# A sum over channels in the attention: two float32r products of split squares instead of one in float32

## The chip, the cores and the metric

One core of a Trainium2 chip runs the kernel. The metric is device time in microseconds, lower is better: the median of the runs. Beside it one execution is profiled, which tells what each engine did when.

## The reference

A hybrid decoder layer on 256 tokens of 1024 channels, all in float32: a SwiGLU feed-forward block, then a Mamba-2 branch and a differential-attention branch side by side, merged by sigmoid gates, then a second feed-forward block. What is changed lies in the attention branch:

```python
p = jax.nn.softmax(s, axis=-1)
attn = p[:, :, 0] - lam * p[:, :, 1]
return jnp.einsum('bhqk,bkhe->bqhe', attn.astype(v.dtype), v)
...
out = out.transpose(1, 0, 2, 3, 4).reshape(b, L, H, DA_V_DIM)
out = rmsnorm(out, subln_g) * (1.0 - lam_init)
return out.reshape(b, L, DA_WIDTH) @ w_branch
```

There are 8 heads. Each has two softmaxes over scores of 64 channels, and 128 output channels, over which `rmsnorm` takes the mean of the squares.

## The kernel before

Large products are done in float32r with split operands. A float32 tile is rounded to `hi` by a cast on ScalarE (L162 for weights, L186 for activations), `lo` = value - `hi` is made on VectorE (L163, L187), and a product is then three float32r products: hi by hi, hi by lo, lo by hi (L196, L197 and L199 in `mm_t`). Weights stream in from DRAM through three `raw` buffers and are split ahead of their use.

After the first feed-forward block the main stream on TensorE is one projection after another, each through `mm_t`: `pxs` and `pz` for the Mamba branch, `pq` and `pk` for queries and keys, `pgt` for the gates, `pws` (Mamba branch output) and `pwd` (attention branch output, which reads the attention's result `oh`, `ol`). Small work of the branches is added between these projections by `Background`: a generator such as `att_work` yields estimates in microseconds and is advanced after each projection. In this part of the kernel no hand-written order is kept on the engines: the framework's scheduler places the instructions of each engine, and so decides between which projection products the small ones stand.

`att_work` handles the heads in four pairs `hp`. For each head:

- `psc` (L833, L834): the scores. For each of the two softmaxes m the 64 channels of m lie on 64 of the 128 rows of the array; each m has one product of 128 columns (first block of queries) and one of 256. They are in float32.
- L835 adds the ALiBi bias on VectorE; L839 and L841 find the negated maxima; the exponentials run on ScalarE (L241); L850 to L855 normalise and subtract on VectorE.
- `pa` (L860): three transposes on TensorE, copied to `aT` (L863).
- `po` (L866, L867): the product with the values, in float32. A pair of heads shares one `po` tile, 128 channels by 2 heads x 256 tokens.

Then, once for each pair: the squares `sqo` of `po` on ScalarE (L869), their sum over the 128 channels, which is a product `pno` with a 128x128 tile of ones in float32 (L871), logarithm and exponential on ScalarE (both through L241), the scaling on VectorE (L875), and the split into `oh` and `ol` (L186, L187). The next head's `psc` does not depend on this. After the last pair stands an activation table load (L234) on ScalarE for the part that follows.

`k2` is a pool of 7 buffers of 2 KB a partition, from which `aT` (one for a head) and `sqo` come. `bg` is a pool of 5 PSUM banks, from which `psc`, `pa`, `po` and `pno` come. A float32 matmul runs as two passes, and the profile shows each pass as a matmul of its own with a weight load.

Of the kernel before, what the change touches and what calls it, by code (L numbers as in the profile page):

```python
# [14 lines left out]
F32 = mybir.dt.float32  # L15
F32R = mybir.dt.float32r
# [8 lines left out]
P = 128  # L25
T = 256
# [19 lines left out]
def tile_hybrid_layer(ctx: ExitStack, tc: tile.TileContext, x, ffn1_pre_g, ffn1_w_gate, ffn1_w_up,  # L46
# [4 lines left out]
    nc = tc.nc  # L51
    const = ctx.enter_context(tc.tile_pool(name="const", bufs=1))
# [4 lines left out]
    def k4(shape, name, dt=F32):  # L57
        return sb.tile(shape, dt, tag="k4", name=name, bufs=K4_BUFS)

    def k3(shape, name, dt=F32):  # L60
        return sb.tile(shape, dt, tag="k3", name=name, bufs=K3_BUFS)

    def k2(shape, name, dt=F32):
        return sb.tile(shape, dt, tag="k2", name=name, bufs=K2_BUFS)
# [4 lines left out]
    def tiny(n, name):  # L69
        return sb.tile([P, n], F32, tag=f"tiny{n}", name=name, bufs=10)  # L70
# [9 lines left out]
    def bg(shape, name):  # L80
        return ps.tile(shape, F32, tag="bg", name=name, bufs=5)
# [103 lines left out]
    def split(hi, lo, src):  # L185
        nc.scalar.copy(hi, src)  # L186
        nc.vector.tensor_sub(lo, src, hi.bitcast(F32))  # L187
# [52 lines left out]
    def act(*args, **kw):  # L240
        a = nc.scalar.activation(*args, **kw)  # L241
        if act_fence[0] is not None:
            tc.add_manual_dep(a.ins, act_fence[0], order, reason="activation table")
        act_since.append(a.ins.name)
# [35 lines left out]
    nc.gpsimd.memset(nhalf, -0.5)  # L280
    ones = const.tile([P, P], F32, name="ones")
    nc.gpsimd.memset(ones, 1.0)

    pw = bg([P, P], "warm")

# [535 lines left out]
    def att_work():  # L821
        for hp in range(4):
            po = bg([P, 2, T], f"po{hp}")
            for i in range(2):
                hd = hp * 2 + i
                qh = qT[hd // 4][:, hd % 4, :]
                kh = kT[hd // 4][:, hd % 4, :]

                s = k3([P, 2, 3 * P], f"s{hd}")
                for m in range(2):  # L830
                    ms = slice(m * 64, (m + 1) * 64)
                    psc = bg([P, 3 * P], f"psc{hd}{m}")
                    nc.tensor.matmul(psc[:, :P], qh[ms, :P], kh[ms, :P], start=True, stop=True)  # L833
                    nc.tensor.matmul(psc[:, P:], qh[ms, P:], kh[ms, :], start=True, stop=True)  # L834
                    nc.vector.scalar_tensor_tensor(s[:, m, :], dneg, 2.0 ** -(hd + 1), psc, ALU.mult, ALU.add)  # L835
                yield 0.9
                nm = tiny(6, f"nm{hd}")
                nmv = nm.rearrange("p (m b) -> p m b", b=3)
                nc.vector.tensor_reduce(nm, s.rearrange("p m (b k) -> p (m b) k", k=P), AX.X, ALU.max,  # L839
                                        negate=True)  # L840
                nc.vector.tensor_tensor(nmv[:, :, 1], nmv[:, :, 1], nmv[:, :, 2], ALU.min)  # L841
                sm = tiny(4, f"sm{hd}")
                smv = sm.rearrange("p (m b) -> p m b", b=2)
                blk = (slice(0, P), slice(P, 3 * P))
                for m in range(2):
                    for qb in range(2):
                        act(s[:, m, blk[qb]], s[:, m, blk[qb]], AF.Exp, bias=nmv[:, m, qb:qb + 1],
                            accum_out=smv[:, m, qb:qb + 1])
                yield 1.0
                nc.vector.reciprocal(sm, sm)  # L850
                nc.vector.tensor_scalar(smv[:, 1, :], smv[:, 1, :], nlam, None, ALU.mult)
                for qb in range(2):
                    s0 = s[:, 0, blk[qb]]
                    nc.vector.tensor_scalar(s0, s0, smv[:, 0, qb:qb + 1], None, ALU.mult)
                    nc.vector.scalar_tensor_tensor(s0, s[:, 1, blk[qb]], smv[:, 1, qb:qb + 1], s0, ALU.mult,  # L855
                                                   ALU.add)

                pa = bg([P, 3 * P], f"pa{hd}")
                for i3 in range(3):
                    nc.tensor.transpose(pa[:, i3 * P:(i3 + 1) * P], s[:, 0, i3 * P:(i3 + 1) * P], ident)  # L860
                yield 1.3
                aT = k2([P, 3 * P], f"aT{hd}")
                nc.scalar.copy(aT, pa)  # L863
                hs = slice((hd % 4) * P, (hd % 4 + 1) * P)
                vh = vt[hd // 4]
                nc.tensor.matmul(po[:, i, :], vh[:, 0, hs], aT[:, :T], start=True, stop=False)  # L866
                nc.tensor.matmul(po[:, i, P:], vh[:, 1, hs], aT[:, T:], start=False, stop=True)  # L867
            sq = k2([P, 2, T], f"sqo{hp}")
            nc.scalar.activation(sq, po, AF.Square)  # L869
            pn = bg([P, 2, T], f"pno{hp}")  # L870
            nc.tensor.matmul(pn.rearrange("p a b -> p (a b)"), ones, sq.rearrange("p a b -> p (a b)"),  # L871
                             start=True, stop=True)
            act(sq, pn, AF.Ln, scale=1.0 / P, bias=eps_c)
            act(sq, sq, AF.Exp, scale=-0.5)
            nc.vector.scalar_tensor_tensor(sq, po, g8, sq, ALU.mult, ALU.mult)  # L875
            if hp % 2 == 0:
                oh[hp // 2] = k4([P, 4, T], f"oh{hp}", F32R)
                ol[hp // 2] = k4([P, 4, T], f"ol{hp}", F32R)
            o = (hp % 2) * 2
            split(oh[hp // 2][:, o:o + 2, :], ol[hp // 2][:, o:o + 2, :], sq)  # L880
            yield 1.3
# [46 lines left out]
    for c in range(4):  # L928
# [11 lines left out]
        back.run(BG_US)  # L940

    back.add(att_work())

    def gates(half):
# [100 lines left out]
```

## Time and profile before

| | |
|---|---|
| median of 3 runs | 768.17 us (767.91 to 768.85) |
| profiled execution, own time | 768.8 us |
| its span (first to last instruction) | 766.0 us |
| granted TensorE clock, mean | 0.999 |
| TensorE matmul busy | 751.8 us (98%) |
| VectorE busy | 522.5 us (68%) |
| ScalarE busy | 441.7 us (58%) |
| attention with `psc` to the last `pno` | about 430 to 524 us after the span's start |

In a row of a timeline the columns are: start, duration (both us), engine, line, operation, tile written <- tiles read, shapes, and how many equal ones were merged; in brackets the idle time of the engine before it and what ended it. In a row of a group, durations are minimum/median/maximum in ns. Matmuls are pipelined and overlap, so their starts tell what they hold TensorE for, and their durations don't. In a row of waits: who waited, at which line, for whom; us in total, times, longest.

### The profile page before, as it was taken

How to read it: one execution, taken by the hardware profiler on the slowest of the kernel's cores; microseconds unless marked ns; L12 is line 12 of the kernel's file. 1: busy time of each engine (PE TensorE's matmuls, PEld its weight loads, DVE VectorE, ACT ScalarE, POOL GpSimd, SP SyncE). 2: the span in 40 equal slices, each digit the busy share in tenths (PEclk: the TensorE clock that was granted, in tenths of full speed). 3: DMA queues.
4: the chain of work that ended last, by engine and by line, in shares of the span. 5: the costliest groups of instructions: out<-in, count | busy, mean ns of one | idle time of the engine just before them, and what ended most of it. 6: DMA issues, size and time to landing. Idle time of an engine off the chain costs nothing.

```text
span 766.0 us, 11904 instructions
## 1 busy us (share of the span) xinstructions
PE 751.8 (98%) x4811; PEld 668.9 (87%) x4811; DVE 522.5 (68%) x815; ACT 441.7 (58%) x721; POOL 32.7 (4%) x73
## 2 busy tenths in 40 slices
PE   8899999999999999999999999999999999999996
PEld 6688888888889999899999988989988888888885
DVE  5586677654577888887868777676785767666612
ACT  7475566553566565666836767665573656555511
POOL 3300000000200000000000000000011000000000
PEclk9999999999999999999999999999999999999999
DMA  9576665586253638465535554436481676545801
GB/s 322 131 237 204 220 220 219 172 297 219 62 165 113 214 119 267 145 219 177 182 110 172 160 164 143 133 114 217 171 296 56 200 240 194 173 169 186 296 0 55
DMA packets 104199, 136.97 MB, mean 179 GB/s; under 512 B 2668, under 2 KB 88784, under 8 KB 104144
## 3 DMA queue, kind: packets, MB, share of 16 engines
q1 hardware_dynamic: 101728, 129.51, 51.4%
q0 software_dynamic: 2112, 6.18, 2.6%
q8 instruction: 37, 0.61, 0.3%
q10 hardware_dynamic: 304, 0.53, 0.2%
q14 instruction: 18, 0.15, 0.1%
HBM read 135.13 MB, written 1.08 MB: 178 GB/s over the span
## 4 chain that ended last, share of the span: by engine, by line
PE 88%; DVE 4%; ACT 3%; issue 1%; POOL 0%; DVEq 0%; POOLq 0%; ACTq 0%
PE acc_f L422 16%; PE pup_f L212 9%; PE pg_f L212 9%; PE pn_f L227 4%; PE pg_f L211 4%; PE pup_f L211 4%; PE pn_mx L227 3%; PE acc_mx L422 3%; PE pxs L197 2%; PE pxs L199 2%; PE pxs L196 2%; PE pz L196 2%; PE pz L199 2%; PE pz L197 2%; PE pgt L199 1%; PE pgt L196 1%
## 5 line engine op out<-in xcount | busy, mean ns | idle before, releaser
L163 DVE TENSOR_TENSOR wlo<-raw,whi 128x1024 fp32r<-128x1024 f32 (+1 forms) x246 | 291.2, 1211 | 47.5 <-ACT whi L162 47.1
L162 ACT CAST whi<-raw 128x1024 fp32r<-128x1024 f32 (+1 forms) x246 | 247.1, 1042 | 52.8 <-PE acc_f L422 18.4
L212 PE MATMUL pg_f<-u_f,whi 128*128 128x512 f32 x288 | 101.2, 396 | 0.0
L212 PE MATMUL pup_f<-u_f,whi 128*128 128x512 f32 x288 | 101.1, 396 | 0.0
L211 PE MATMUL pg_f<-u_f,wlo 128*128 128x256 f32 x252 | 70.6, 280 | 0.0
L211 PE MATMUL pup_f<-u_f,wlo 128*128 128x256 f32 x252 | 70.4, 279 | 0.0
L212 PEld LDWEIGHTS pg_f<-u_f,whi 128*128 128x128 f32 x288 | 53.0, 188 | 9.6
L212 PEld LDWEIGHTS pup_f<-u_f,whi 128*128 128x128 f32 x288 | 52.8, 188 | 9.7
L422 PE MATMUL acc_f<-whi,gh_f 128*128 128x512 f32 x176 | 58.2, 390 | 0.0
L422 PE MATMUL acc_f<-wlo,gh_f 128*128 128x512 f32 x176 | 58.2, 390 | 0.0
L422 PE MATMUL acc_f<-whi,gl_f 128*128 128x512 f32 x176 | 58.1, 389 | 0.0
L211 PEld LDWEIGHTS pup_f<-u_f,wlo 128*128 128x128 f32 x252 | 47.6, 189 | 1.6
L211 PEld LDWEIGHTS pg_f<-u_f,wlo 128*128 128x128 f32 x252 | 47.6, 189 | 1.6
L216 DVE TENSOR_TENSOR su_f<-pup_f,su_f 128x256 f32<-128x256 f32 x36 | 15.2, 421 | 39.7 <-ACT su_f L215 39.7
L422 PEld LDWEIGHTS acc_f<-wlo,gh_f 128*128 128x128 f32 x176 | 33.0, 188 | 6.9
L422 PEld LDWEIGHTS acc_f<-whi,gl_f 128*128 128x128 f32 x176 | 33.0, 188 | 6.8
L422 PEld LDWEIGHTS acc_f<-whi,gh_f 128*128 128x128 f32 x176 | 33.1, 188 | 6.7
L197 PE MATMUL pws<-yl,whi 128*128 128x256 f32 x128 | 32.8, 291 | 0.0
L196 PE MATMUL pz<-u_mx,whi 128*128 128x256 f32 x128 | 32.3, 289 | 0.0
L196 PE MATMUL pgt<-u_mx,whi 128*128 128x256 f32 x128 | 32.2, 288 | 0.0
L196 PE MATMUL pws<-yh,whi 128*128 128x256 f32 x128 | 32.0, 285 | 0.0
L197 PE MATMUL pgt<-u_mx,whi 128*128 128x256 f32 x128 | 31.8, 284 | 0.0
(305 smaller groups left out, 1574.1 us busy)
## 6 DMA issues: line engine op xcount, KB each, us to landing
raw<-in_w_in_dram SPq DMA_DIRECT2D x40, 1024.0 KB, 5.5
raw<-in_ffn_w_down_dram SPq DMA_DIRECT2D x22, 1024.0 KB, 5.0
raw<-in_ffn_w_gate_dram SPq DMA_DIRECT2D x20, 1024.0 KB, 5.9
raw<-in_ffn_w_up_dram SPq DMA_DIRECT2D x20, 1024.0 KB, 5.7
raw<-in_ssd_w_branch_dram SPq DMA_DIRECT2D x8, 1024.0 KB, 5.3
acb<-acd POOLq DMA_DIRECT2D x8, 512.0 KB, 4.0
raw<-in_da_w_branch_dram SPq DMA_DIRECT2D x4, 1024.0 KB, 5.3
raw<-in_w_out_dram SPq DMA_DIRECT2D x4, 1024.0 KB, 6.2
```

Of the source, the lines that this page charges most:

```text
L162: nc.scalar.copy(hi[:, js, :], r[:, q * nj + j:q * nj + j + n, :])
L163: nc.vector.tensor_sub(lo[:, js, :], r[:, q * nj + j:q * nj + j + n, :], hi[:, js, :].bitcast(F32))
L196: nc.tensor.matmul(acc[m], wh(j)[:, cs], ah(k0 + j), start=first and j == 0, stop=False)
L197: nc.tensor.matmul(acc[m], wh(j)[:, cs], al(k0 + j), start=False, stop=False)
L199: nc.tensor.matmul(acc[m], wl(j)[:, cs], ah(k0 + j), start=False, stop=last and j == KD - 1)
L211: nc.tensor.matmul(acc[:, :T], wl(j)[:, cs], ah(j), start=False, stop=False)
L212: nc.tensor.matmul(acc, wh(j)[:, cs], ahl(j), start=j == 0, stop=j == KD - 1)
L216: nc.vector.tensor_tensor(dst[:, m, :], acc[:, :T], dst[:, m, :], ALU.add)
L227: nc.tensor.matmul(acc, a(k0 + j), b(j), start=first and i == 0, stop=last and i == 11)
L422: nc.tensor.matmul(acc[b][q], x_[:, ts], w_(kt)[:, halves[q]], start=i == 0 and kt == 0 and x_ is ah and w_ is wh, stop=i == n - 1 and kt ...
```

## The change

A float32r copy of the tile of ones, `ones_r`, is made once on VectorE at the start. For each pair of heads the squares `sq` are split on VectorE: a copy into a float32r tile `sqh` (hi), and a subtraction `sql` = `sq` - `sqh` (lo), both 128x512 and from the pool `k2`. The sum over channels is then two float32r products with `ones_r`, accumulated in the same `pno` tile: hi first, then lo. Everything before and behind stays as it was in the text of the program; the scheduler places all of it anew.

```diff
     ones = const.tile([P, P], F32, name="ones")
     nc.gpsimd.memset(ones, 1.0)
+    ones_r = const.tile([P, P], F32R, name="ones_r")
+    nc.vector.tensor_copy(ones_r, ones)
...
             sq = k2([P, 2, T], f"sqo{hp}")
             nc.scalar.activation(sq, po, AF.Square)
             pn = bg([P, 2, T], f"pno{hp}")
-            nc.tensor.matmul(pn.rearrange("p a b -> p (a b)"), ones, sq.rearrange("p a b -> p (a b)"),
-                             start=True, stop=True)
+            sqh, sql = [k2([P, 2 * T], f"sqo{hp}{x}", F32R) for x in "hl"]
+            sqf = sq.rearrange("p a b -> p (a b)")
+            nc.vector.tensor_copy(sqh, sqf)
+            nc.vector.tensor_sub(sql, sqf, sqh.bitcast(F32))
+            for i, part in enumerate((sqh, sql)):
+                nc.tensor.matmul(pn.rearrange("p a b -> p (a b)"), ones_r, part, start=i == 0, stop=i == 1)
             act(sq, pn, AF.Ln, scale=1.0 / P, bias=eps_c)
             act(sq, sq, AF.Exp, scale=-0.5)
             nc.vector.scalar_tensor_tensor(sq, po, g8, sq, ALU.mult, ALU.mult)
```

The changed program, built, differs in the order of instructions only from the first of these places to the first `pwd` products (and by the copy of the ones at the start of VectorE). With the number of TensorE instructions of each kind in the program's order, around the four places: before, the one `pno` product follows `po` after 7, 6, 6 and 7 float32r products, and at the first three `psc` (L833, L834, L833, L834) follows it directly. After, the hi product follows `po` after 10, 10, 10 and 16 float32r products; at the first three come `psc` L833, L834, then the lo product, then `psc` L833, L834; at the fourth six float32r products and the lo product. On VectorE the copy and the subtraction stand directly behind each other, except at the fourth place, where a product with the gates (L973) lies between.

## The prediction

> **What bounds the kernel now.** I read the page first, then the sums of the stretch in which the attention runs, then the rows of the tiles `pno` and `psc` in order of time, and last the waits there. The profiled execution took 768.8 us, 2.8 us more than its span; the runs have a median of 768.17 us, so it lies 0.6 us above it, within their spread. All sums are made against the span of 766.0 us and carried over to the median.
>
> ```profile
> PE 751.8 (98%) x4811; PEld 668.9 (87%) x4811; DVE 522.5 (68%) x815; ACT 441.7 (58%) x721; POOL 32.7 (4%) x73
> PE 88%; DVE 4%; ACT 3%; issue 1%; POOL 0%; DVEq 0%; POOLq 0%; ACTq 0%
> ```
>
> The first row is busy time by engine, the second the shares of the chain that ended last. TensorE is both times the bound. The attention shows no exception:
>
> ```profile
> core 0: us, PE busy (x) PEld busy (x) DVE busy (x) ACT busy (x) POOL busy (x), PEclk, DMA share, GB/s
> 430.00:530.00 100.00, 98.32 (x767) 90.00 (x766) 72.96 (x129) 70.86 (x138) 0.00 (x0) 1.00 0.47 156
> ```
>
> So a microsecond of TensorE issue saved or added here is a microsecond of the end, while VectorE has 27 us of room in these 100 us and its additions cost only where TensorE waits for them. Four places count, one per pair of heads `hp`.
>
> **TensorE: the sum over channels.** The fourth place (`hp` 3) shows the old product by itself among float32r products:
>
> ```profile
> 522.76 0.28 PE L196 MATMUL pws<-yh,whi 128*128 128x256 f32 x1
> 522.89 1.12 PE L871 MATMUL pno<-sqo,ones 128*128 128x512 f32 x2
> 523.46 0.68 PE L197 MATMUL pws<-yl,whi 128*128 128x256 f32 x1
> 523.97 0.28 PE L196 MATMUL pws<-yh,whi 128*128 128x256 f32 x1
> ```
>
> Columns are start, duration, engine, line. Starts tell more than durations, since matmuls overlap. From 522.76 to 523.97 are 1.21 us, and two 256-column float32r products stand in it besides the old one. These start 0.12 us apart when nothing disturbs them (453.21, 453.32, 453.44 below), so the float32 product, two passes, holds TensorE for 1.21 - 0.24 = 0.97 us. A float32r product of 512 columns:
>
> ```profile
> 552.21 7.96 PE acc_mx L422 x35
> ```
>
> 35 of them in 7.96 us are 0.227 us each, two are 0.45. At `hp` 3 the change saves 0.97 - 0.45 = 0.52 us.
>
> **TensorE: what the new products come between.** At `hp` 0, 1 and 2 the old product is followed at once by the next head's scores, `psc`. Their two halves (m = 0, 1) use 64 rows of the array each:
>
> ```profile
> 453.21 0.28 PE L197 MATMUL pgt<-u_mx,whi 128*128 128x256 f32 x1
> 453.32 0.28 PE L196 MATMUL pgt<-u_mx,whi 128*128 128x256 f32 x1
> 453.44 0.28 PE L197 MATMUL pgt<-u_mx,whi 128*128 128x256 f32 x1
> 453.56 0.28 PE L196 MATMUL pgt<-u_mx,whi 128*128 128x256 f32 x1
> 453.70 1.13 PE L871 MATMUL pno<-sqo,ones 128*128 128x512 f32 x2
> 454.75 0.50 PE L833 MATMUL psc<-k,q 64*128 64x128 f32 x4
> 455.08 0.61 PE L834 MATMUL psc<-k,q 64*128 64x256 f32 x4
> 455.62 0.39 PE L197 MATMUL pgt<-u_mx,whi 128*128 128x256 f32 x1
> 455.84 0.28 PE L196 MATMUL pgt<-u_mx,whi 128*128 128x256 f32 x1
> ```
>
> In the program the order is L833 and L834 of the first half, then both of the second, each two passes. Here all four passes of L833 start before the first of L834: the halves run side by side. In the built changed program they no longer stand together. At each of these three places the order is: hi product, first half of `psc`, lo product, second half. A lo product that takes all 128 rows stands between the halves, so they can't lie over each other. What a half costs by itself the trace doesn't show; the pair by itself it does:
>
> ```profile
> 430.00 0.64 PE L199 MATMUL pgt<-u_mx,wlo 128*128 128x256 f32 x4
> 430.57 0.50 PE L833 MATMUL psc<-k,q 64*128 64x128 f32 x4
> 430.89 0.61 PE L834 MATMUL psc<-k,q 64*128 64x256 f32 x4
> 431.43 0.39 PE L196 MATMUL pgt<-u_mx,whi 128*128 128x256 f32 x1
> 431.65 0.28 PE L197 MATMUL pgt<-u_mx,whi 128*128 128x256 f32 x1
> ```
>
> The last L199 starts at 430.36 (three steps of 0.12). From there to 431.65 are 1.29 us, less 0.24 for two undisturbed products: 1.05 us for a pair, its way in and out included. As its halves lie over each other, a half alone costs the same 1.05 at the upper end. At the lower end it costs what its columns cost in the old product: 0.97 us for 2 x 512 columns, so 0.73 for 2 x 128 + 2 x 256.
>
> One place before: 453.56 to 455.84 is 2.28, less 0.24, so 2.04 us for the old product and the pair. After: 2 x 1.05 + 0.45 = 2.55 at the upper end, 2 x 0.73 + 0.45 = 1.91 at the lower. The place changes by -0.13 to +0.51 us. I take 0.5, because that row is of the very operation, with its entry and exit. TensorE in sum: 3 x 0.5 - 0.52 = +1.0 us (bounds -0.9 and +1.0). The change saves 0.5 us four times and loses about 1.0 three times.
>
> "TensorE: Matmul & The Clock Gate" of the Trainium skill, section "Step-by-step: what each phase is for", says that matmuls stay in program order and only weight loads are pulled ahead. By that rule the halves would already run one after the other and parting them would be free. The rows above speak against it for these two halves. "TensorEngine Tiling (Array Packing)" of the same skill, "Key Properties", says that a change of tiling mode drains the array; the parted order has two more such changes at each place, which is the direction of my sum and no part of it.
>
> **VectorE and the waits.** Added are four copies and four subtractions of 128x512, and one copy of 128x128 at the start, where nothing waits for it. Nearest rows (for a copy: one tensor in, SBUF to SBUF):
>
> ```profile
> L366 DVE TENSOR_SCALAR un_f<-h,r_f x3: 479/501/598, 16.2 to 581.1; 128x512 f32<-128x512 f32 x3
> L187 DVE TENSOR_TENSOR ol<-sqo,oh x4: 680/682/691, 458.4 to 527.9; 128x512 fp32r<-128x512 f32 x4
> ```
>
> 0.50 + 0.68 = 1.18 us a place, 4.7 in all, against 27 us of room. They lie between ScalarE's square and the products, so TensorE may wait. What it waits for now:
>
> ```profile
> PE pa L860 <- DVE s L855: 1.6, 4, 0.6
> PEld pa L860 <- DVE s L855: 0.6, 1, 0.6
> PEld pno L871 <- ACT sqo L869: 0.4, 2, 0.2
> ```
>
> At `hp` 0 the square starts at 453.05 and takes 0.60; VectorE is idle then:
>
> ```profile
> 453.05 0.60 ACT L869 ACTIVATE sqo<-po 128x512 f32<-128x512 f32 x1
> 455.71 0.56 DVE L835 SCALAR_TENSOR_TENSOR s<-dneg,psc 128x384 f32<-128x384 f32 x1 [3.57 <-PE psc L834]
> ```
>
> The copy ends at 453.65 + 0.50 = 454.15. The built order puts three more float32r products ahead of the hi product, so TensorE is there at 453.70 + 0.36 = 454.06: it waits 0.1, and the main projections queued behind it wait too. The lo part comes 0.68 later, which the first half of `psc` (0.73 at least) covers. At `hp` 1 and 2 a split of weights (L163, 1.22 us) may stand before the copy; four more products are the cover there, so 0 to 0.6. I take 0.15 a place, 0.6 in all, less the 0.4 for `pno` that goes: +0.2. The waits for `pa`, 2.2 us now, sit behind the softmax of the head whose second half comes later; `pa` is moved too, so I leave them as they are, with -1 to +1.5 as their bounds.
>
> The square of `hp` 1:
>
> ```profile
> 475.62 0.60 ACT L869 ACTIVATE sqo<-po 128x512 f32<-128x512 f32 x1
> ```
>
> The two new tiles of a place take buffers from the pool `k2`: five a place instead of three, of seven, so a buffer comes round at the next place or the one after it, some 23 us on (453.05 to 475.62), when its last reader, the split of `oh`, is done; nothing is costed for it.
>
> Sum: +1.0 + 0.2 = +1.2 us. Span 767.2, time 768.17 + 1.2 = 769.4 us.
>
> **Rivals.** A, the sum above: 769.4. B, program order: if the halves run one after the other as the program has them, parting them is free and only the products count, 4 x -0.52 + 0.2 = -1.9, so 766.3. Against it stands that two halves one after the other would take 2 x 0.73 = 1.46 us by the lower price, and the whole pair takes 1.05. By the rule of the skill's first page above it would come out as B.
>
> C, the last place turns into a wait. In the built order the last lo product stands six products ahead of the first `pwd`, where the old one stood 43 ahead. From it to the first `pwd` that reads `hp` 3's `oh` are 6 + 21 products (the scheduler has put eight of the second `pwd` in between), 27 x 0.12 = 3.2 us. What must happen meanwhile, as it is now:
>
> ```profile
> 522.74 1.98 ACT L162 CAST whi<-raw 128x1024 fp32r<-128x1024 f32 x2
> 524.62 0.69 ACT L241 ACTIVATE sqo<-pno,eps_c 128x512 f32<-128x512 f32 x1
> 525.34 0.63 ACT L241 ACTIVATE sqo<-sqo 128x512 f32<-128x512 f32 x1
> 525.99 1.28 ACT L234 ACT_TABLE_LOAD   x1
> 527.28 0.62 ACT L186 CAST oh<-sqo 128x512 fp32r<-128x512 f32 x1
> ```
>
> From the first Ln (524.62) to the end of the cast (527.90) are 3.3 us, and the product itself adds 0.23: 3.5, 0.3 too late. Now casts of weights hold the Ln up by 0.6 us more; if one (1.0 us) does so there, `pwd` waits 1.3, with two of them 2.3. Price 0.3 to 2.3; from 0.4 us on it makes the whole slower by over 0.2%. With 1.9 it is 771.3. Against it: the scheduler moved those eight products to cover just this, and one cast has gone ahead of the square.
>
> **How the numbers follow.** A has 0.60, B 0.08, C 0.32. 0.2% is 1.5 us, about what a measurement of this kernel can tell from no change. A at +1.2 with 0.7 either way is within it in about three quarters of its cases and above in the rest; C is above in most. Faster 0.07, same 0.50, slower 0.43. The range: from 767.5 (A with the lower price of the halves, -0.9 + 0.2) to 771.3 (C); B and the longest waits of C lie outside.
>
> **What would show it.** Right: at `hp` 0 to 2 two `psc` groups of L833 x2, L834 x2 instead of x4, with a `pno` start between, and about 2.5 us from the last float32r product ahead to the second after; `pno` as eight products of one pass each, at `hp` 3 two of them in 0.45 us; TensorE waits of a few tenths for the hi copy. Wrong: the second half starts beside the lo product, or a half alone takes clearly under 0.9 us (then less than +1.2, or faster); or a wait over 0.5 us of `pwd` for `oh` (C), or waits for `pa` in sum more than 1.5 us from 2.2.

## The result, and the profile after

The changed kernel takes 770.26 us (median of 7 runs, 769.98 to 770.45), the kernel before 767.91 us beside it (7 runs, 767.54 to 768.85). The ratio is 1.0028 with a 95% interval of 1.0017 to 1.0040: slower by 2.35 us or 0.28%, over the 0.2% that the prediction took for what a measurement can tell. The profiled execution took 770.4 us with a span of 768.5 us.

First the page of the changed kernel: busy time by engine, and the shares of the chain that ended last. Then the sums of the stretch in which the attention runs.

```profile
PE 754.0 (98%) x4811; PEld 670.3 (87%) x4811; DVE 527.1 (69%) x824; ACT 441.7 (57%) x721; POOL 32.6 (4%) x73
PE 89%; DVE 4%; ACT 2%; issue 1%; POOL 0%; DVEq 0%; POOLq 0%; ACTq 0%
...
430.00:530.00 100.00, 98.63 (x753) 90.03 (x751) 74.78 (x134) 67.60 (x134) 0.00 (x0) 1.00 0.44 142
```

TensorE is the bound as before, and its busy time has grown by 2.2 us. VectorE has 4.6 us more, about the 4.7 forecast. These totals do not say where the end moved. The starts do: the first `psc` product starts at 430.57 before and 430.68 after, the first `acc_mx` product (L422, now L424) at 552.05 and 554.44. So the stretch from the one to the other takes 121.48 us before and 123.76 after, +2.28 us. What comes behind it takes 214.0 us before and 214.1 after. Nearly the whole difference lies in the attention's stretch, and each experiment below is given with the length of that stretch.

Now one place, `hp` 0, in the changed kernel's timeline (start, duration, engine, line):

```profile
453.79 0.43 DVE L875 CAST sqo0h<-sqo 128x512 fp32r<-128x512 f32 x1 [1.53 <-ACT sqo L871]
...
454.03 0.28 PE L197 MATMUL pgt<-u_mx,whi 128*128 128x256 f32 x1
...
454.36 0.47 PE L878 MATMUL pno<-sqo0h,ones_r 128*128 128x512 f32 x1
454.76 0.48 PE L835 MATMUL psc<-k,q 64*128 64x128 f32 x2
455.08 0.59 PE L836 MATMUL psc<-k,q 64*128 64x256 f32 x2
455.61 0.49 PE L878 MATMUL pno<-sqo0l,ones_r 128*128 128x512 f32 x1
456.03 0.48 PE L835 MATMUL psc<-k,q 64*128 64x128 f32 x2
456.36 0.59 PE L836 MATMUL psc<-k,q 64*128 64x256 f32 x2
456.88 0.38 PE L196 MATMUL pgt<-u_mx,whi 128*128 128x256 f32 x1
457.10 0.28 PE L197 MATMUL pgt<-u_mx,whi 128*128 128x256 f32 x1
```

`psc` now comes in groups of two passes instead of four, with a `pno` product between them. One half takes from 454.76 to 455.61, 0.85 us, the other from 456.03 to 456.88, 0.85 again. Before, the whole pair took 0.86 (430.57 to 431.43 in the prediction's rows). So a half alone costs as much as the pair. The place, from the last float32r product ahead to the second one behind, takes 3.07 us, less 0.24 for two undisturbed products: 2.83. In it the hi product starts 0.33 behind its forerunner instead of 0.12, since the copy on VectorE ends only at 453.79 + 0.43 = 454.22: 0.21 us of waiting. Without it the place costs 2.62, where it was 2.04 before.

The last place, `hp` 3, has two products in the float32r stream, each 0.23 us from start to next start:

```profile
529.05 0.40 PE L878 MATMUL pno<-sqo3h,ones_r 128*128 128x512 f32 x1
529.28 0.28 PE L196 MATMUL pws<-yh,whi 128*128 128x256 f32 x1
...
530.00 0.39 PE L878 MATMUL pno<-sqo3l,ones_r 128*128 128x512 f32 x1
530.23 0.63 PE L199 MATMUL pws<-yh,wlo 128*128 128x256 f32 x4
```

What TensorE waits for in the changed kernel from 430 to 560 us (in sum, times, longest), and one of ScalarE's waits, first of before and then of after; behind them the products at which the two new waits end, in order of time:

```profile
ACT sqo L241 <- PE pno L871: 2.7, 3, 1.2
```

```profile
ACT sqo L241 <- PE pno L878: 7.1, 4, 2.5
PEld pa L862 <- DVE s L857: 1.4, 3, 0.6
PE pa L862 <- DVE s L857: 0.7, 3, 0.4
PEld pws L196 <- ACT whi L162: 0.6, 1, 0.6
PEld pwd L196 <- ACT oh L186: 0.4, 1, 0.4
```

```profile
508.73 0.88 PE L199 MATMUL pws<-yh,wlo 128*128 128x256 f32 x6
509.98 0.39 PE L196 MATMUL pws<-yh,whi 128*128 128x256 f32 x1 [0.36 <-ACT whi L162]
510.20 0.28 PE L197 MATMUL pws<-yl,whi 128*128 128x256 f32 x1
...
533.33 0.28 PE L196 MATMUL pwd<-oh,whi 128*128 128x256 f32 x1
533.82 0.39 PE L196 MATMUL pwd<-oh,whi 128*128 128x256 f32 x1 [0.22 <-ACT oh L186]
534.04 0.28 PE L197 MATMUL pwd<-ol,whi 128*128 128x256 f32 x1
```

Where line and releaser agree, the rows of weight loads (PEld) and of matmuls (PE) can tell of the same gap, so sizes are taken from the starts. Two of the waits are new: `pws` for a cast of weights (`whi`), and `pwd` for `oh`. The last of the six L199 starts at 509.33 (five steps of 0.12). So in starts the first wait is a gap of 0.64 us where 0.12 is usual, and the second one of 0.50 from 533.33; in both the next step takes 0.22, another 0.10 more. They cost 0.62 and 0.48 us. ScalarE stands 7.1 us at the logarithm for `pno`, where it stood 2.7.

### The profile page after: what moved, and what is told of

It reads as the page before. It is cut to its first block, busy times and chain, and to the rows that moved or that the text cites. A ratio compares the mean times of both kernels' runs of the same rounds, so it can differ in the third digit from the quotient of the medians.

```text
span 768.5 us, 11916 instructions
## 1 busy us (share of the span) xinstructions
PE 754.0 (98%) x4811; PEld 670.3 (87%) x4811; DVE 527.1 (69%) x824; ACT 441.7 (57%) x721; POOL 32.6 (4%) x73
## 4 chain that ended last, share of the span: by engine, by line
PE 89%; DVE 4%; ACT 2%; issue 1%; POOL 0%; DVEq 0%; POOLq 0%; ACTq 0%
PE acc_f L424 16%; PE pup_f L212 9%; PE pg_f L212 9%; PE pn_f L227 4%; PE pg_f L211 4%; PE pup_f L211 4%; PE pn_mx L227 3%; PE acc_mx L424 3%; PE pxs L199 2%; PE pxs L197 2%; PE pxs L196 2%; PE pz L196 2%; PE pz L199 2%; PE pz L197 2%; PE pws L196 2%; PE pws L197 1%
## 5 line engine op out<-in xcount | busy, mean ns | idle before, releaser
L424 PE MATMUL acc_f<-whi,gh_f 128*128 128x512 f32 x176 | 58.1, 390 | 0.0
L424 PE MATMUL acc_f<-whi,gl_f 128*128 128x512 f32 x176 | 58.1, 389 | 0.0
L424 PE MATMUL acc_f<-wlo,gh_f 128*128 128x512 f32 x176 | 58.1, 389 | 0.0
L424 PEld LDWEIGHTS acc_f<-wlo,gh_f 128*128 128x128 f32 x176 | 33.0, 188 | 6.9
L424 PEld LDWEIGHTS acc_f<-whi,gl_f 128*128 128x128 f32 x176 | 33.0, 188 | 6.8
L424 PEld LDWEIGHTS acc_f<-whi,gh_f 128*128 128x128 f32 x176 | 33.0, 188 | 6.7
L196 PE MATMUL pgt<-u_mx,whi 128*128 128x256 f32 x128 | 32.5, 289 | 0.0
L215 ACT COPY su_f<-pup_f 128x256 f32<-128x256 f32 x36 | 13.3, 370 | 32.3 <-PE pup_f L212 32.1
```

Source lines behind the costliest of these rows:

```text
L196: nc.tensor.matmul(acc[m], wh(j)[:, cs], ah(k0 + j), start=first and j == 0, stop=False)
L215: nc.scalar.copy(dst[:, m, :], acc[:, T:])
L424: nc.tensor.matmul(acc[b][q], x_[:, ts], w_(kt)[:, halves[q]], start=i == 0 and kt == 0 and x_ is ah and w_ is wh, stop=i == n - 1 and kt ...
```

## The experiments

Every ratio is against the kernel before, run on the same chip. The stretch is the time between the starts of the first `psc` and of the first `acc_mx` product in the profiled execution.

| kernel | us, median | ratio, 95% interval | stretch, us |
|---|---|---|---|
| before | 767.7 to 767.9 | 1 | 121.48 |
| the change | 770.26 | 1.0028 (1.0017 to 1.0040) | 123.76 |
| halves together | 768.30 | 1.0001 (0.9992 to 1.0010) | 121.92 |
| halves parted by a float32r product, 8 heads | 774.96 | 1.0090 (1.0076 to 1.0104) | 128.58 |
| the same product behind the pair | 769.23 | 1.0017 (1.0008 to 1.0026) | 122.89 |
| halves parted by a float32 product | 776.19 | 1.0108 (1.0094 to 1.0122) | 129.84 |
| halves together, cast ahead of the Ln | 768.59 | 1.0009 (1.0000 to 1.0018) | 121.80 |
| before, cast ahead of the Ln | 768.07 | 1.0003 (0.9994 to 1.0011) | 121.88 |
| the change, cast ahead of the Ln | 769.40 | 1.0024 (1.0015 to 1.0033) | 123.09 |
| hi product alone | 765.11 | 0.9959 (0.9947 to 0.9971) | 118.68 |
| VectorE's part alone | 768.72 | 1.0016 (1.0005 to 1.0026) | 122.20 |
| `hp` 3 alone | 767.70 | 1.0000 (0.9991 to 1.0009) | 121.35 |
| scores first | 766.87 | 0.9992 (0.9983 to 1.0001) | 120.44 |
| scores first, lo before hi | 767.25 | 0.9989 (0.9980 to 0.9998) | 120.40 |

**Halves together.** The change, with one order added:

```diff
-                    nc.tensor.matmul(psc[:, :P], qh[ms, :P], kh[ms, :P], start=True, stop=True)
+                    f = nc.tensor.matmul(psc[:, :P], qh[ms, :P], kh[ms, :P], start=True, stop=True)
+                    if i == 0 and m == 0 and lo_mm is not None:
+                        tc.add_manual_dep(f.ins, lo_mm.ins.name, order, reason="halves together")
...
-                nc.tensor.matmul(pn.rearrange("p a b -> p (a b)"), ones_r, part, start=i == 0, stop=i == 1)
+                lo_mm = nc.tensor.matmul(pn.rearrange("p a b -> p (a b)"), ones_r, part, start=i == 0, stop=i == 1)
```

> The change as it is, with one thing more: the first scores product of the next head is ordered behind the lo product, so that the two halves of psc stand together again at the three places hp 0 to 2 (hi, 4 to 12 projection products, lo, then the pair). Theory 1 (the parted halves are the loss): a place holds TensorE for 1.05 us of the pair and 2 x 0.23 us of products in the float32r stream, 1.51 instead of 2.04 before, some 0.2 us of waiting for the hi copy at each place stays, and so does the wait for oh at the end (0.4): 3 x -0.33 - 0.51 + 0.4 = -1.1 us, 766.8 us (766.0 to 767.6), faster than the kernel before by 0.14%, and 3.5 us under the change. Rival 2 (the halves do not lie over each other, or the loss comes from VectorE's new work and the waits that the new order brought): parting was free, the time stays within 1 us of the change, 769.3 to 771.3.

Measured: 768.30 us, between the two ranges. `hp` 0 in its timeline:

```profile
453.95 0.28 PE L197 MATMUL pgt<-u_mx,whi 128*128 128x256 f32 x1
454.28 0.47 PE L881 MATMUL pno<-sqo0h,ones_r 128*128 128x512 f32 x1
...
455.06 0.39 PE L881 MATMUL pno<-sqo0l,ones_r 128*128 128x512 f32 x1
455.38 0.50 PE L836 MATMUL psc<-k,q 64*128 64x128 f32 x4
...
456.24 0.38 PE L196 MATMUL pgt<-u_mx,whi 128*128 128x256 f32 x1
456.47 0.28 PE L197 MATMUL pgt<-u_mx,whi 128*128 128x256 f32 x1
```

From 453.95 to 456.47 are 2.52 us with six float32r products of the projection in them (four lie between hi and lo), so 1.80, and 1.59 without the 0.21 for the hi copy. The change has 2.62 there: this order is worth 1.0 us at `hp` 0. With the wait for the hi copy, which is gone at `hp` 1, the three places hold TensorE 3.3 us less, and the wait of `pwd` for `oh` (0.5) goes too. The kernel got 2 us faster (1.84 by the stretch). The products of `pa` hold TensorE 1.0 longer, by the starts, and the wait of `pws` for `whi` grows by 1.0:

```profile
PEld pws L196 <- ACT whi L162: 1.5, 1, 1.5
```

**Halves parted in the kernel before.** Nothing of the change is in these three kernels but a tile `ones_r`. At all eight heads one product of 128 columns on all 128 rows is ordered between the halves, or behind them:

```diff
-                    psc = bg([P, 3 * P], f"psc{hd}{m}")
+                    psc = bg([P, 4 * P], f"psc{hd}{m}")
...
+                    if m == 0:        # behind the pair: m == 1
+                        fill = nc.tensor.matmul(psc[:, 3 * P:], ones_r, ones_r, start=True, stop=True)
+                        tc.add_manual_dep(fill.ins, g.ins.name, order, reason="order")
```

In the parted ones the second half is ordered behind `fill`; the float32 one takes `ones` for `ones_r`.

> The kernel before, with one float32r product of 128 columns on all 128 rows (ones by ones, into columns of psc that nobody reads) ordered between the two halves of psc at all eight heads. Theory 1: a half alone costs what the pair costs (0.85 us), and two more changes of type (0.2 to 0.27 together) come with it: 8 x 1.05 to 1.15 = +8.4 to +9.2 us over the same product behind the pair, so about 777 us. Rival 2 (halves run one after the other anyway): only the two changes of type and the product count, 8 x 0.3 = +2.4 us at most, 770.3.

> The same added float32r product as in the parted kernel, but ordered behind the second half of psc, at all eight heads: the control for the product itself. By both theories 8 x 0.06 to 0.12 us, +0.5 to +1.0, 768.4 to 769.0 us; order elsewhere may differ by a few projection products.

> As the parted kernel, but the product between the halves is float32 (two passes of 128 columns), so no change of type comes between the halves: what is left is the lost overlap alone and the product (0.13 to 0.25 us by the 0.97 us of 1024 columns and by the 0.12 us a short pass). Theory 1 with the overlap as the main part: 8 x (0.85 - 0.1 + 0.2), +7 to +8 us over the kernel before, 775 to 776. If the changes of type were the main part instead: +1 to +2.5 us, 769 to 770.5.

Measured: 774.96, 769.23 and 776.19 us, 2 below, 0.2 above and 0.2 above what theory 1 gave. The first head's pair, with the float32r product behind it, then between, then with the float32 product between:

```profile
429.92 0.76 PE L199 MATMUL pgt<-u_mx,wlo 128*128 128x256 f32 x5
430.61 0.50 PE L836 MATMUL psc<-k,q 64*128 64x128 f32 x4
...
431.48 0.33 PE L839 MATMUL psc<-ones_r 128*128 128x128 f32 x1
...
431.81 0.28 PE L197 MATMUL pgt<-u_mx,whi 128*128 128x256 f32 x1
```

```profile
429.97 0.76 PE L199 MATMUL pgt<-u_mx,wlo 128*128 128x256 f32 x5
430.66 0.49 PE L836 MATMUL psc<-k,q 64*128 64x128 f32 x2
...
431.51 0.33 PE L841 MATMUL psc<-ones_r 128*128 128x128 f32 x1
431.76 0.48 PE L836 MATMUL psc<-k,q 64*128 64x128 f32 x2
...
432.85 0.27 PE L197 MATMUL pgt<-u_mx,whi 128*128 128x256 f32 x1
```

```profile
430.53 0.49 PE L836 MATMUL psc<-k,q 64*128 64x128 f32 x2
...
431.38 0.49 PE L841 MATMUL psc<-ones 128*128 128x128 f32 x2
431.80 0.48 PE L836 MATMUL psc<-k,q 64*128 64x128 f32 x2
```

The last L199 starts four steps of 0.12 after the row's start: 430.40 and 430.45. So the pair with the product behind it holds TensorE for 431.81 - 430.40 - 0.24 = 1.17 us, the parted one for 432.85 - 430.45 - 0.24 = 2.16. Parting costs 0.99 us a head, near the 1.05 to 1.15 expected and far from the 0.3 of program order. With float32 between them, where no type changes, the halves stand just as far apart: 430.53 to 431.38 is 0.85 again, and the product itself takes 0.42 instead of 0.25. It is the lost overlap that costs, not the change of type. Between the two float32r kernels the time differs by 5.7 us, though, not by 8 x 0.99 = 7.9: the waits of `pa` for the softmax, 1.8 us in the matmuls' own row with the product behind the pair, are gone when the halves are parted, and by the starts the products of `pa` hold TensorE 2.3 us less. What TensorE issues longer, the softmax gets as time.

The Trainium skill, "TensorE: Matmul & The Clock Gate", section "The mechanism", says that products on different row groups run at the same time, and that matmuls nevertheless start and end strictly in order. The first half of it is what these rows show (pair 0.86 us, half 0.85). The second is not: with four passes of the 128-column product ahead of all passes of the 256-column one, the second half's first product has overtaken the first half's second.

**A cast ahead of the logarithm.** One chunk of weights more is split before `hp` 2's Ln is traced, in three kernels (halves together, before, the change):

```diff
+            if hp == 2:
+                split_to(len(splits) + 1)
             act(sq, pn, AF.Ln, scale=1.0 / P, bias=eps_c)
```

> The version with the halves together, and besides it one chunk of weights more is split ahead of hp 2's logarithm, so that no weight cast stands on ScalarE behind the wait for pno there. Theory 1 now has a second term: with the halves together 1.5 us were left in one wait of pws for whi (after 506.76), since ScalarE stood 1.87 us at the Ln for pno (1.22 before) with the cast queued behind it. By it that wait goes and nothing takes its place: 768.3 - 1.5 = 766.8 us (766.4 to 767.4). Rival: the stretch is bound by the softmax chain, and what is won at the cast comes back as waits for pa: 767.9 to 768.6.

> The kernel before with the same chunk split ahead of hp 2's logarithm and nothing else: the control. Before has no wait for whi over 0.1 us in the attention, so theory 1 expects no gain: 767.4 to 768.4 us. If an earlier cast is worth something by itself (rival), it comes out near 766.5.

> The change as it is (halves parted), with one chunk of weights more split ahead of hp 2's logarithm. In the change pws waited 0.5 us for whi there. If that wait is a loss by itself: 770.3 - 0.5 = 769.7 us. If, as with the halves together, the time comes back at the end as a wait of pwd for oh: 770.0 to 770.8.

Why a cast comes late is seen on ScalarE's timeline, first of before, then of the change:

```profile
501.73 0.69 ACT L241 ACTIVATE sqo<-pno,eps_c 128x512 f32<-128x512 f32 x1 [1.22 <-PE pno L871]
...
504.42 1.05 ACT L162 CAST whi<-raw 128x1024 fp32r<-128x1024 f32 x1
```

```profile
504.72 0.69 ACT L241 ACTIVATE sqo<-pno,eps_c 128x512 f32<-128x512 f32 x1 [2.45 <-PE pno L878]
...
508.89 1.03 ACT L162 CAST whi<-raw 128x1024 fp32r<-128x1024 f32 x1
```

ScalarE stands 1.22 us for `pno` before and 2.45 after, with the cast queued behind. The cast comes 4.5 us later on the run's clock, though the place itself is only 1.8 us late (its square starts at 499.91 before and at 501.67 after); 1.2 of the other 2.7 us are the longer wait, and the built order has also put the exponentials of the next head in between.

The order differs in one thing more. Counted from the first `psc`, the product that waits for this cast is the 481st of the projections' products. The first `pno` product of `hp` 2 stands behind the 437th of them before, behind the 447th in the change and behind the 463rd with the halves together. There the cast comes 2.9 us later than before (at 507.29), of which only 0.65 are ScalarE's longer wait for `pno` (1.87 for 1.22), less than in the change; and yet TensorE waits longer for it.

Measured: with the halves together 768.59 us, no gain. No wait of TensorE for `whi` is left, and `pwd` waits for `oh` instead:

```profile
PEld pwd L196 <- ACT oh L186: 1.0, 1, 1.0
```

The rival was right that it would come back, and wrong on where: not at `pa` but at the tail. The earlier start of `pwd` (527.34 against 529.48) met an `oh` that was 1.6 us later (its cast ends at 533.07 against 531.47). The edit moved more than the cast: the first `pno` product of `hp` 3 now stands behind the 631st projection product, seven of them `pwd`'s own, where it stood behind the 605th. So it is not shown what an earlier cast alone would bring with the halves together. The kernel before gains nothing from the earlier cast (768.07, as expected). With the halves parted it comes out at 769.40, nearer the expected 769.7 than the rival's 770.0 to 770.8, and the stretch is 0.67 shorter, with the wait for `whi` gone and the one for `oh` as it was; the intervals of the two times overlap, so of this one only the stretch speaks.

**The hi product alone.** The square is written in float32r at once:

```diff
-            sq = k2([P, 2, T], f"sqo{hp}")
-            nc.scalar.activation(sq, po, AF.Square)
+            sqr = k2([P, 2, T], f"sqr{hp}", F32R)
+            nc.scalar.activation(sqr, po, AF.Square)
...
+            nc.tensor.matmul(pn.rearrange("p a b -> p (a b)"), ones_r, sqr.rearrange("p a b -> p (a b)"),
+                             start=True, stop=True)
```

> The product alone: ScalarE's square writes a float32r tile and one float32r product sums it; VectorE's split and the lo product are left out, so the squares enter rounded. Halves of psc stay together, and the Ln waits no longer than before. Theory 1: 4 x (0.227 - 0.97) = -3.0 us, 764.9 us, up to 766.3 if the waits for pa take back part, as they gave back part when TensorE had more to do (the parted kernel lost 5.7 us where its places had grown by 8.3). Rival (the product's length hardly counts beside the waits): 767.3 to 768.

Measured: 765.11 us, 0.9959 of before, within the expected range. By the starts the four places hold TensorE 2.5 us less and the products of `pa` 0.3; the whole gain of the shorter product comes through. The place:

```profile
453.47 0.28 PE L196 MATMUL pgt<-u_mx,whi 128*128 128x256 f32 x1
453.60 0.50 PE L875 MATMUL pno<-sqr,ones_r 128*128 128x512 f32 x1
454.03 0.50 PE L836 MATMUL psc<-k,q 64*128 64x128 f32 x4
...
455.12 0.28 PE L196 MATMUL pgt<-u_mx,whi 128*128 128x256 f32 x1
```

1.65 - 0.24 = 1.41 us for 2.04. Of it the product takes 0.43 (453.60 to 454.03), not 0.23 as in its own stream. The float32 product behind it can't be the whole reason: with the halves together the lo product, also directly ahead of `psc`, took 0.32 (455.06 to 455.38). It is the fastest of these kernels. Its squares are rounded, so it is no replacement of equal precision.

**VectorE's part alone.** The split is made and not read:

```diff
+            nc.vector.tensor_copy(sqh, sqf)
+            nc.vector.tensor_sub(sql, sqf, sqh.bitcast(F32))
             nc.tensor.matmul(pn.rearrange("p a b -> p (a b)"), ones, sq.rearrange("p a b -> p (a b)"),
                              start=True, stop=True)
```

> VectorE's part alone: the copy and the subtraction are made, nobody reads them, and the sum over channels stays one float32 product of the whole squares. Theory 1: 4.5 us of VectorE work in the room that it has, nothing for TensorE to wait for: 767.6 to 768.4 us. Rival (VectorE's work delays the softmax and the weights' lo): +1 us or more, 768.8 and up.

Measured: 768.72 us, above the expected range and below the rival's. The stretch is 0.72 longer. No single wait holds it: tenths of a microsecond at several `pa`, at `hp` 3's square and at `oh`. The scheduler has also placed the sums of `hp` 2 and 3 later, behind the 452nd and the 595th projection product where before they stood behind the 437th and the 581st. So it is not shown whether VectorE's time costs the 0.7 us or the order that came with it.

**`hp` 3 alone.** `if hp < 3:` keeps the float32 product.

> The change at hp 3 alone; hp 0 to 2 keep the float32 product. Theory 1: -0.5 us for the product, no parting; in the built order 22 products of pws and some of pwd stand between the lo product and the first use of oh, where the change had 6, so the wait for oh (0.4 in the change) goes too: 767.1 to 767.7 us. Rival C as the prediction had it (VectorE's split and the casts of weights hold the Ln up, pwd waits for oh 0.4 us or more): 768 and up.

Measured: 767.70 us, at the upper end of the expected range, ratio 1.0000. Its profiled execution reaches the attention 1.5 us late, so only the stretch compares: -0.13 us. The saved 0.5 is there in the rows, and most of it is given back: a wait of `pwd` for `ol` (0.24 by the starts) and a lo product that waits for VectorE (0.08 by the starts, and 0.1 more to its next).

**Scores first.** Two products in float32r need not cost the overlap. In the last two kernels the next head's `psc` is traced ahead of the sum and ordered right behind `po`, so that it covers VectorE's split:

```diff
+            def finish(hp=hp, po=po, sq=sq):
+                ...    # pno, split, products, Ln, Exp, scaling, oh and ol
+            pending = finish
...
+                if i == 0 and pending is not None:    # behind this head's psc
+                    pending()
                 yield 0.9
```

> The whole change (hi, lo, two float32r products), but the next head's scores are traced ahead of it and ordered right behind po: both halves of psc run together while VectorE splits the squares, and hi and lo stand behind them among the projection's products. Theory 1 (places): po and psc as one float32 group 1.66 us, 2 x 0.23 for hi and lo, no wait for the hi copy: 2.12 instead of 2.68 at hp 0 to 2, -0.5 at hp 3, so -2.2 us: 765.6 us if no new wait comes. Rival (ScalarE's queue and the softmax chain take it back, as they did where the halves were together and the wait moved from whi to the end): 767 to 768.5.

Measured: 766.87 us, between the two expectations. By the stretch 1.04 us of the expected 2.2 are won; hi, right behind the pair, waits for VectorE:

```profile
453.18 0.61 PE L839 MATMUL psc<-k,q 64*128 64x256 f32 x4
454.17 0.47 PE L884 MATMUL pno<-sqo0h,ones_r 128*128 128x512 f32 x1 [0.38 <-DVE sqo0h L881]
```

The last kernel has `(sql, sqh)` for `(sqh, sql)`:

> As the kernel with psc first, with the two products in the other order: lo first, then hi. Both then stand side by side some 12 projection products behind psc (32 at hp 3), where hi alone stood at once behind psc and TensorE waited for VectorE. Theory 1 (places): those waits, 0.4 us at hp 0 and hp 2 and 0.3 at hp 1 for lo, go: 766.9 - 0.8 = 766.1 us (765.7 to 766.8), faster than the kernel before by 0.2%. Rival (the Ln comes later by the products in between, and ScalarE's queue gives the time back at oh or whi): 766.8 to 768.

Measured: 767.25 us, ratio 0.9989 (0.9980 to 0.9998), stretch 120.40. The order bought nothing more: now lo waits 0.2 to 0.4 us at three places. At `hp` 0:

```profile
456.89 0.47 PE L884 MATMUL pno<-sqo0l,ones_r 128*128 128x512 f32 x1 [0.17 <-DVE sqo0l L882]
```

The time lies in the rival's range, but not for the rival's reason: TensorE waits for lo, and not for `oh` or `whi`. The waits moved instead of going. Of the kernels that sum hi and lo this and the one before it are the fastest, 0.4% below the change. Against the kernel before the gain is 0.1%; only the last one's interval leaves out 1, and by so little that, with so many kernels compared, a gain is not shown.

## Why the prediction was right, and where its sum was short

The forecast was +1.2 us, within 0.2% as the likeliest class; measured were +2.35 us, inside the range and over 0.2%, the class that had 0.43. The account of the stretch, by its own steps, measured ones by the starts:

| step | forecast, us | measured, us |
|---|---|---|
| `hp` 3, two products in 0.45 for 0.97 | -0.52 | -0.51 |
| three places, parted halves less the product | +1.53 | +1.74 |
| waits for the hi copy | +0.6 | +0.63 |
| waits of `pno` for the square that go | -0.4 | -0.27 |
| places of `pa` and `po` (waits for the softmax and `aT`) | 0 | -0.4 |
| `pws` for `whi` | none | +0.62 |
| `pwd` for `oh` (rival C) | in C alone | +0.48 |
| sum | +1.2 | +2.3, as in the stretch |

- **The range.** +2.35 lies above A's own band, +1.2 with 0.7 either way. It is inside the range because that reached up to rival C. Two terms that A's sum did not have came, and a third of the other sign, -0.4 at `pa` and `po`, hid a part of them by luck.
- **The parted halves.** Right in mechanism and nearly in size: 2.62 us a place, 2.55 forecast. (The sign of "about 2.5 us" between the starts leaves out the 0.24 for the two undisturbed products and the wait; the starts lie 3.07 apart.) The upper price, a half as dear as the pair, is what the change and the kernels with a product between the halves show (0.85 and 0.85). The 0.07 a place is the longer float32r products: from 454.36 to 454.76 and from 455.61 to 456.03, 0.40 and 0.42 instead of 0.23 each, less what the second half's own entry was priced at.
- **Rival B**, program order with nothing to lose, fell: two kernels that part the halves at all heads with one small product are 7.2 and 8.4 us slower than before, and the control with the float32r product behind the pair only 1.5. The rule of order that B leaned on forbids overtaking, not overlap: by it the second half's first product could still have run beside the first half's second.
- **The waits for the hi copy** are as forecast in sum, but 0.2 at each of the three places instead of 0.1 at one and up to 0.6 at others; the cast took 0.43 us, not 0.50.
- **What the sum lacks is what stands on ScalarE behind the Ln.** The prediction followed VectorE's split to TensorE and let the Ln come later without asking what is queued behind it. A cast of weights stood there and came too late: +0.6 us in the change, +1.6 once the halves were together. In the kernels with the cast moved ahead the wait for `whi` is gone, so the cast's place behind the Ln is its cause. ScalarE's longer wait for `pno` (4.4 us more in sum) explains only a part of the lateness, 1.2 of 4.5 us in the change and 0.65 of 2.9 with the halves together. How the rest divides between the later place and the built order stays open.
- **Rival C was set against A as an alternative, and it is a term.** Its lower price, 0.3, was 3.5 us of work against 3.2 us of cover; 0.37 came at the first product that waited and 0.1 at its next, with no cast of weights ahead of the Ln (ScalarE had waited 1.63 us for `pno` at `hp` 3). It came on top of A, so a sum with both would have been +1.5, and the likeliest class would have stood on the edge.
- **The waits for `pa`** were left as they were; counted as there, by the rows, they are 1.4 + 0.7 = 2.1 for 2.2. By the starts the products of `pa` hold TensorE 0.7 us less than before and those of `po` 0.3 more. The kernels with parted halves show them to be a buffer: they give back about 2 of 8 us.

What stays open: how the 0.7 us of VectorE's part alone divide between its work and the new order, and so how much of the table's small differences belongs to it.

## What to carry to other kernels

Two products on different halves of the array cost as one here (0.86 us the pair, 0.85 one alone) only while they stood next to each other. Before splitting an operand so that a product waits, look in the built order at what the scheduler will put in the gap, and give the pair an order if it must stay one. A longer way to a result is paid by what stands behind it on the engine that waits for it, which may be a cast of weights that has nothing to do with the change. Where a scheduler places everything anew, count in the trace where the work landed before a difference is put down to the edit. List the waits of one change as terms that add up, not as rivals that exclude each other, unless one really takes the other's place.

## What the runs showed of the hardware that was not expected

- A scores half of 64 rows takes 0.85 us alone and the pair of halves 0.86 us: the overlap was complete, where the prediction's lower end had 0.73 for a half.
- A float32r product of 512 columns takes 0.23 us in a float32r stream, 0.31 there when it has just waited for its operand (454.28 to 454.59 with the halves together), and with a float32 product of 64 rows behind it 0.32 (halves together) to 0.43 (hi alone).
- Between the same halves a 128-column product on all rows took 0.25 us in float32r and 0.42 in float32.
